# The rotation of q and k in an encoder kernel, on GpSimd instead of VectorE

## The chip, the cores and the metric

One core of one Trainium2 chip runs the whole program. The metric is the device time in microseconds (us), the median of several executions. The engines are named as the profile names them: PE (TensorE's matmuls), PEld (its weight loads), DVE (VectorE), ACT (ScalarE), POOL (GpSimd), SP (SyncE, which here only issues transfers).

## The reference, cut to what matters

Two residual layers (`DEPTH = 2`) over 256 tokens of width 1024. Each layer normalises its input, multiplies it by one wide matrix `w_in`, and feeds the segments of the product to two branches: a gated delta rule (segments `q_a`, `k_a`, `v_a`, with a short convolution) and a differential softmax attention (`q_b`, `k_b`, `v_b`). Both are gated, projected, merged and projected again. The change concerns the attention's `q_b` and `k_b` alone. Before the scores are formed, the first 16 of the 64 columns of each of 16 sub-heads are rotated by an angle that depends on the token:

```python
def partial_rope(t, cos, sin):
    half = ROPE_DIM // 2                     # 8
    x1 = t[..., :half]
    x2 = t[..., half:ROPE_DIM]
    return jnp.concatenate([x1 * c - x2 * s, x2 * c + x1 * s, t[..., ROPE_DIM:]], axis=-1)

q = partial_rope(q.reshape(bsz, seq, DIFF_HEADS, 2, DIFF_DH), cos, sin) * (DIFF_DH ** -0.5)
k = partial_rope(k.reshape(bsz, seq, DIFF_HEADS, 2, DIFF_DH), cos, sin)
```

## The kernel before, in words

All weights come from memory in blocks of 256 rows by 512 columns, `raw`, and each is split into two numbers whose sum it is: `hi`, a cast on ACT (L308; on DVE for the blocks listed as `turned`), and `lo`, a subtraction on DVE (L310). PE multiplies three times, hi by hi, lo by hi and hi by lo. In `proj_tm` (token-major, 512 columns at a time) these are L324, L325 and L326, in `proj_fm` (feature-major, for the convolution) L385, L387 and L389. PE thus waits for ACT's cast and DVE's subtraction of every block.

`qk_part(s_, i)` makes one half (512 columns, `i` = 0 or 1) of q (`s_` = 0) or k (`s_` = 1). `proj_tm` calls `evac_qk(m, ps)` for each of the two tiles of 128 tokens. That makes 2 layers x 2 x 2 x 2 = 16 tiles. For one tile:

- ACT copies the product from the accumulator to `st` (the tile `stg`, 128x512; L597). `st` has two buffers, and the tag is shared with a few other tiles.
- Four operations rotate it in place: two products with cosines and sines into the scratch tile `r4` (L602, L603; 128 elements per partition each), then a difference and a sum back into the first 16 columns of each group of 64 (L604, L605; 64 elements each, in runs of 8). `r4` has one buffer, so the next tile's L602 waits for this tile's L605. In the profile `r4` is called `r`.
- PE transposes the tile in four blocks (L608) into the bank `qkt`, and ACT writes it, scaled, to `qkT` (L610), which the scores (L1061) read later.

The four halves are made between the segments of the other branch: q half 0 after the first half of the convolution of q, q half 1 after its second half, k half 0 and 1 after the first half of the convolution of v and around the second. While the rotation of a half runs, PE is already in the products of the next segment. Around these places DVE also carries out the convolution's taps (L679, L690) and a substitution (L870, L871), which solves the triangular systems.

POOL has other work there: `turn_blocks` sends the blocks of `A` through memory (transfers L847, L849, L850) and clears `X` (L851, L852); `bounce` sends v's squares, after a transposition on DVE (L135), through memory (L140 out, L142 back). A transfer that POOL issues stands in POOL's queue, and what stands behind it waits until it is issued.

Every engine carries out its instructions in the order in which they stand in its queue. That order is not written out in the source: a scheduler sets it while the program is built, from its own estimates of how long each operation takes, within limits that the source gives (`behind(...)` means issued after a certain instruction, `high_priority` moves work forward).

Of the kernel before, what the change touches and what calls it, by code (L numbers as in the profile page):

```python
# [12 lines left out]
ALU = mybir.AluOpType  # L13
# [36 lines left out]
def hybrid_encoder(  # L50
# [19 lines left out]
    V, S, G, T = nc.vector, nc.scalar, nc.gpsimd, nc.tensor  # L70
# [15 lines left out]
    def bank(name):  # L86
        return ps_m.tile([P, 512], F32, tag="m", name=name)
# [10 lines left out]
    def mid(ap, n):  # L98
        return ap.unsqueeze(1).to_broadcast([ap.shape[0], n] + list(ap.shape[1:]))
# [215 lines left out]
    def proj_tm(act, w, c0, n, evac, nm, places=(None,) * 4, spare=(), later=None, turned=(), between=None,  # L315
                banks=None, held=None, first=(), raws={}):

        accs = (banks or banks2)(f"pp_{nm}")
        for kt, hi, lo in weights(w, c0, n, nm, places, later=later, spare=spare, turned=turned, held=held,
                                  first=first, raws=raws):  # L320
            for m in range(NM):
                ts_ = slice(m * P, (m + 1) * P)
                o = accs[m][:, :n]
                T.matmul(o, act[kt // 4][:, 0, kt % 4, ts_], hi, start=kt == 0, stop=False)  # L324
                T.matmul(o, act[kt // 4][:, 0, kt % 4, ts_], lo, start=False, stop=False)  # L325
                mark["proj"] = T.matmul(o, act[kt // 4][:, 1, kt % 4, ts_], hi, start=False,  # L326
                                        stop=kt == KT - 1).ins
                mark["done", nm, kt] = mark["proj"]
        if between:
            between()  # L330
        for m in range(NM):
            evac(m, accs[m][:, :n])
# [174 lines left out]
    for l in range(DEPTH):  # L507
# [26 lines left out]
        if l == 0:  # L534
# [23 lines left out]
            sin, cos = sincos[:, 0], sincos[:, 1]  # L558
# [35 lines left out]
        def qk_part(s_, i):  # L594
                def evac_qk(m, ps):
                    st = work.tile([P, 512], F32, tag="w2a", name=f"stg{l}{s_}{i}{m}", bufs=2)
                    S.copy(st, ps)  # L597
                    g_ = st.rearrange("p (g e) -> p g e", e=DH)
                    x12 = g_[:, :, 0 : 2 * RD].rearrange("p g (x r) -> p g x r", x=2)
                    both = lambda t_: mid(mid(t_[:, m, :], 2), 8)  # L600
                    r4 = small.tile([P, 2, 8, 2, RD], F32, tag="r4", name=f"r4{l}{s_}{i}{m}", bufs=1)
                    V.tensor_tensor(r4[:, 0], x12, both(cos), ALU.mult)  # L602
                    V.tensor_tensor(r4[:, 1], x12, both(sin), ALU.mult)  # L603
                    V.tensor_tensor(x12[:, :, 0], r4[:, 0, :, 0], r4[:, 1, :, 1], ALU.subtract)  # L604
                    V.tensor_tensor(x12[:, :, 1], r4[:, 0, :, 1], r4[:, 1, :, 0], ALU.add)  # L605
                    pt = bank(f"qkt{l}{m}{s_}{i}")
                    for b in range(4):
                        T.transpose(pt[:, b * P : (b + 1) * P], st[:, b * P : (b + 1) * P], ident)  # L608

                    mark["qkT", m] = S.mul(qkT[i][:, s_, :, m * P : (m + 1) * P],  # L610
                                           pt.rearrange("p (b t) -> p b t", b=4), (DH ** -0.5, 1.0)[s_]).ins
                proj_tm(hT, wl, (C_QB, C_KB)[s_] + 512 * i, 512, evac_qk, f"qk{l}{s_}{i}",
                        turned=(0, 1) if (s_, i) == (0, 1) else ())
# [770 lines left out]
```

## Time and profile before

| | |
|---|---|
| median of 3 executions | 749.98 us (749.95 to 750.64) |
| span of the profiled execution, first to last instruction | 748.5 us |
| PE busy | 739.3 us, 99% |
| PEld busy | 641.7 us, 86% |
| DVE busy | 586.5 us, 78% |
| ACT busy | 481.2 us, 64% |
| POOL busy | 139.5 us, 19% |
| mean granted TensorE clock | 0.998 |

The profile holds one execution. Its span runs from the first to the last instruction; the time of an execution includes what lies around that, and the median is 1.5 us above the span. Busy time is the time in which an engine had an instruction; an engine off the chain that ends last may be idle at no cost. Matmuls overlap, so one takes longer (0.39 us for 512 columns) than the distance to the next (0.23 us).

### The profile page before, as it was taken

Reading aid. Unit: us, or ns where it says so; the run is one execution under the profiler, and the core shown is the slowest. Engines: PE = TensorE matmul, PEld = TensorE weight load, DVE = VectorE, ACT = ScalarE, POOL = GpSimd, SP = SyncE. Lnnn points to the kernel's source line nnn. Section 1 sums busy time; section 2 is a strip of 40 time slices with the busy share of each in tenths; the row PEclk is TensorE's granted clock in tenths of the full one; section 3 lists DMA queues with packets and bytes.
Section 4 is the critical chain, followed back from the end, with each engine's and each line's share of the span. In section 5 each row is a group of like instructions: output and inputs, shape, how many; then the busy total and the mean of one; then the engine's idle time right before and its main releaser. Section 6 shows DMA issues by size and latency. Waiting matters only on the chain.

```text
span 748.5 us, 13917 instructions
## 1 busy us (share of the span) xinstructions
PE 739.3 (99%) x5176; PEld 641.7 (86%) x5176; DVE 586.5 (78%) x1109; ACT 481.2 (64%) x1022; POOL 139.5 (19%) x221
## 2 busy tenths in 40 slices
PE   8999999999999999999999999999999999999996
PEld 6999889987888889888889899889778888998885
DVE  8696898999985965578668779999999679537782
ACT  6757875667876576645456578555687757566552
POOL 6004110112023440100000150202110425301000
PEclk9999999999999999999999999999999999999999
DMA  8754566776667462567674466767666748335641
GB/s 260 239 170 169 170 179 198 209 211 193 208 177 186 145 184 84 171 200 247 199 232 133 128 192 180 219 176 230 195 171 195 197 133 229 95 114 201 220 141 57
DMA packets 73734, 135.46 MB, mean 181 GB/s; under 512 B 12944, under 2 KB 13921, under 8 KB 73666
## 3 DMA queue, kind: packets, MB, share of 16 engines
q1 hardware_dynamic: 64750, 113.65, 50.6%
q0 software_dynamic: 7936, 19.35, 8.7%
q10 hardware_dynamic: 980, 1.58, 0.6%
q8 instruction: 41, 0.67, 0.4%
q14 instruction: 27, 0.22, 0.1%
HBM read 125.53 MB, written 9.01 MB: 180 GB/s over the span
## 4 chain that ended last, share of the span: by engine, by line
PE 95%; ACT 2%; issue 1%; DVE 1%; DMA 1%; SPq 0%; POOLq 0%; POOL 0%; DVEq 0%; ACTq 0%
PE pp_vb L369 4%; PE pp_qk L325 4%; PE pp_qk L326 3%; PE pp_qk L324 3%; PE sc L1061 2%; PE pp_o L369 2%; PE pf_k L385 2%; PE pp_za L325 2%; PE pf_v L385 2%; PE pf_v L389 2%; PE pp_gb L324 2%; PE pp_gb L325 2%; PE pp_zb L324 2%; PE pf_q L387 2%; PE pf_k L387 2%; PE pf_v L387 2%
## 5 line engine op out<-in xcount | busy, mean ns | idle before, releaser
L325 PE MATMUL pp_qk<-lo_qk,hT 128*128 128x512 f32 x128 | 50.5, 395 | 0.3
L326 PE MATMUL pp_qk<-hi_qk,hT 128*128 128x512 f32 x128 | 50.0, 390 | 0.0
L310 DVE TENSOR_TENSOR lo_qk<-raw_qk,hi_qk 128x1024 fp32r<-128x1024 f32 x32 | 39.1, 1222 | 11.6 <-ACT hi_qk L308 11.4
L324 PE MATMUL pp_qk<-hi_qk,hT 128*128 128x512 f32 x128 | 45.1, 393 | 0.0
L308 ACT CAST hi_qk<-raw_qk 128x1024 fp32r<-128x1024 f32 x28 | 29.4, 1049 | 23.4 <-PE pp_qk L326 12.4
L1071 ACT ACTIVATE es<-sc,mx 128x256 f32<-128x256 f32 x64 | 29.6, 474 | 19.5 <-DVE mx L1069 19.5
L387 PE MATMUL pf_q<-hT,hi_q 128*128 128x256 f32 x128 | 36.1, 286 | 0.0
L385 PE MATMUL pf_k<-hT,hi_k 128*128 128x256 f32 x128 | 36.1, 287 | 0.0
L385 PE MATMUL pf_v<-hT,hi_v 128*128 128x256 f32 x128 | 35.9, 285 | 0.0
L387 PE MATMUL pf_v<-hT,hi_v 128*128 128x256 f32 x128 | 35.8, 284 | 0.0
L385 PE MATMUL pf_q<-hT,hi_q 128*128 128x256 f32 x128 | 35.8, 284 | 0.0
L387 PE MATMUL pf_k<-hT,hi_k 128*128 128x256 f32 x128 | 35.8, 284 | 0.0
L310 DVE TENSOR_TENSOR lo_pb<-raw_pb,hi_pb 128x1024 fp32r<-128x1024 f32 x16 | 19.6, 1225 | 20.5 <-ACT hi_pb L308 20.2
L389 PE MATMUL pf_q<-hT,lo_q 128*128 128x256 f32 x128 | 35.2, 288 | 0.0
L389 PE MATMUL pf_v<-hT,lo_v 128*128 128x256 f32 x128 | 34.6, 288 | 0.0
L389 PE MATMUL pf_k<-hT,lo_k 128*128 128x256 f32 x128 | 34.3, 284 | 0.0
L308 ACT CAST hi_pa<-raw_pa 128x1024 fp32r<-128x1024 f32 x16 | 16.8, 1053 | 22.3 <-PE pp_pa L326 16.1
L679 DVE SCALAR_TENSOR_TENSOR cvq<-pf_q,cw,cvq 128x254 f32<-128x254 f32 (+1 forms) x64 | 30.0, 479 | 0.9 <-ACT cvq L675 0.3
L679 DVE SCALAR_TENSOR_TENSOR cvv<-pf_v,cw,cvv 128x254 f32<-128x254 f32 (+1 forms) x64 | 30.1, 482 | 0.1
L679 DVE SCALAR_TENSOR_TENSOR cvk<-pf_k,cw,cvk 128x254 f32<-128x254 f32 (+1 forms) x64 | 29.0, 478 | 1.3 <-ACT cvk L675 0.6
L325 PEld LDWEIGHTS pp_qk<-lo_qk,hT 128*128 128x128 f32 x128 | 24.0, 188 | 6.6 <-DVE lo_qk L310 1.6
L310 DVE TENSOR_TENSOR lo_pa<-raw_pa,hi_pa 128x1024 fp32r<-128x1024 f32 x16 | 19.6, 1224 | 11.1 <-ACT hi_pa L308 11.1
(414 smaller groups left out, 2542.2 us busy)
## 6 DMA issues: line engine op xcount, KB each, us to landing
raw_qk<-in_w_in_dram SPq DMA_DIRECT2D x32, 512.0 KB, 3.8
raw_k<-in_w_in_dram SPq DMA_DIRECT2D x16, 512.0 KB, 4.7
raw_q<-in_w_in_dram SPq DMA_DIRECT2D x16, 512.0 KB, 3.7
raw_v<-in_w_in_dram SPq DMA_DIRECT2D x16, 512.0 KB, 3.8
raw_zb<-in_w_in_dram SPq DMA_DIRECT2D x16, 512.0 KB, 3.7
raw_za<-in_w_in_dram SPq DMA_DIRECT2D x16, 512.0 KB, 3.7
raw_ga<-in_w_in_dram SPq DMA_DIRECT2D x16, 512.0 KB, 4.4
raw_pb<-in_w_pb_dram SPq DMA_DIRECT2D x16, 512.0 KB, 3.8
```

The source lines that it names most:

```text
L308: high = (V.tensor_copy if kp in turned else S.copy)(hi[:, :, :n], raw[:, :, :n]).ins
L310: mark[nm, kp] = high, V.tensor_tensor(lo[:, :, :n], raw[:, :, :n], hi[:, :, :n].bitcast(F32), ALU.subtract).ins
L324: T.matmul(o, act[kt // 4][:, 0, kt % 4, ts_], hi, start=kt == 0, stop=False)
L325: T.matmul(o, act[kt // 4][:, 0, kt % 4, ts_], lo, start=False, stop=False)
L326: mark["proj"] = T.matmul(o, act[kt // 4][:, 1, kt % 4, ts_], hi, start=False, stop=kt == KT - 1).ins
L369: mark["proj"] = T.matmul(o, act[kt // 4][:, pa, kt % 4, ts_], ws[kt][1 + pw], start=kt == 0 and n_ == 0, stop=kt == KT - 1 and n_ == 2).ins
L385: T.matmul(o, hi[:, cs], act[kt // 4][:, 0, kt % 4, :], start=first, stop=False, skip_group_check=True)
L387: T.matmul(o, hi[:, cs], act[kt // 4][:, 1, kt % 4, :], start=False, stop=False, skip_group_check=True)
L389: T.matmul(o, lo[:, cs], act[kt // 4][:, 0, kt % 4, :], start=False, stop=done, skip_group_check=True)
L679: V.scalar_tensor_tensor(ca[:, o0:o1], acc[:, b, o0 + sft : o1 + sft], cw[:, j, cb : cb + 1], ca[:, o0:o1], ALU.mult, ALU.add)
L1061: mm = T.matmul(sp[n][:, qt * SEQ : (qt + 1) * SEQ], qkT[h // 4][rows, 0, h % 4, qt * P : (qt + 1) * P], qkT[h // 4][rows, 1, h % 4, :], s ...
L1071: S.activation(es[:, n, qt, :], spv[:, qt, :], AF.Exp, bias=mx[:, n, qt : qt + 1], accum_out=s_all[:, h, n, qt : qt + 1])
```

## The change

The four operations of the rotation are issued by `G` (POOL) and no longer by `V` (DVE). Nothing else in the source is changed.

```diff
                     r4 = small.tile([P, 2, 8, 2, RD], F32, tag="r4", name=f"r4{l}{s_}{i}{m}", bufs=1)
-                    V.tensor_tensor(r4[:, 0], x12, both(cos), ALU.mult)
-                    V.tensor_tensor(r4[:, 1], x12, both(sin), ALU.mult)
-                    V.tensor_tensor(x12[:, :, 0], r4[:, 0, :, 0], r4[:, 1, :, 1], ALU.subtract)
-                    V.tensor_tensor(x12[:, :, 1], r4[:, 0, :, 1], r4[:, 1, :, 0], ALU.add)
+                    G.tensor_tensor(r4[:, 0], x12, both(cos), ALU.mult)
+                    G.tensor_tensor(r4[:, 1], x12, both(sin), ALU.mult)
+                    G.tensor_tensor(x12[:, :, 0], r4[:, 0, :, 0], r4[:, 1, :, 1], ALU.subtract)
+                    G.tensor_tensor(x12[:, :, 1], r4[:, 0, :, 1], r4[:, 1, :, 0], ALU.add)
                     pt = bank(f"qkt{l}{m}{s_}{i}")
```

The scheduler sets a new order on all engines. Two places matter below. First, PE at the transposes of the second tile of k's half 0 in layer 0 (bank `qkt_1724`, tile `stg_1717`), in the products of v's second half (`pf_v`); lines with - stand so before, with + now:

```order
 L389 MATMUL pf_v_1740<-hT_0_126,lo_v_1773 128x256
 L385 MATMUL pf_v_1741<-hT_0_126,hi_v_1772 128x256
+L608 MATMUL qkt_1724<-ident,stg_1717 128x128 x4
 L387 MATMUL pf_v_1741<-hT_0_126,hi_v_1772 128x256
 L389 MATMUL pf_v_1741<-hT_0_126,lo_v_1773 128x256
...
 L385 MATMUL pf_v_1741<-hT_1_127,hi_v_1832 128x256
 L387 MATMUL pf_v_1741<-hT_1_127,hi_v_1832 128x256
-L608 MATMUL qkt_1724<-ident,stg_1717 128x128 x4
 L389 MATMUL pf_v_1740<-hT_1_127,lo_v_1833 128x256
 L385 MATMUL pf_v_1740<-hT_1_127,hi_v_1832 128x256
```

The four transposes stand 33 products earlier than before. Of the other seven sets of transposes in layer 0, one stands where it stood, one stands 5 products later, and five stand earlier, by 1 to 24 rows; among these are the second tile of q's half 0 (`qkt_1117`), 20 products of 256 columns earlier, and the second tile of k's half 1 (`qkt_2012`), 12 products of 512 columns earlier.

Second, POOL's queue at the two tiles of k's half 1 in layer 0 (tiles `stg_1992` and `stg_2005`, scratch `r_1994` and `r_2007`):

```order
 L142 DMA tb_v_1622<-bnc_v_1624 32x4x128 x4
+L602 TENSOR_TENSOR r_1994<-stg_1992,sincos 128x128
+L603 TENSOR_TENSOR r_1994<-stg_1992,sincos 128x128
+L604 TENSOR_TENSOR stg_1992<-r_1994 128x8x8
+L605 TENSOR_TENSOR stg_1992<-r_1994 128x8x8
+L602 TENSOR_TENSOR r_2007<-stg_2005,sincos 128x128
+L603 TENSOR_TENSOR r_2007<-stg_2005,sincos 128x128
 L140 DMA bnc_v_1881<-tb_v_1879 128x512
+L604 TENSOR_TENSOR stg_2005<-r_2007 128x8x8
+L605 TENSOR_TENSOR stg_2005<-r_2007 128x8x8
 L142 DMA tb_v_1879<-bnc_v_1881 32x4x128 x4
```

The second tile's last two operations now stand behind a transfer (L140) that is issued only when DVE has transposed v's squares (L135). In layer 1 both places look the same.

## The prediction

> **What bounds the kernel now.** I read the page's busy times first, then the chain that ended last, then PE's idle time by stages, then what PE waited for.
>
> ```profile
> PE 739.3 (99%) x5176; PEld 641.7 (86%) x5176; DVE 586.5 (78%) x1109; ACT 481.2 (64%) x1022; POOL 139.5 (19%) x221
> PE 95%; ACT 2%; issue 1%; DVE 1%; DMA 1%; SPq 0%; POOLq 0%; POOL 0%; DVEq 0%; ACTq 0%
> 0.00:15.00 15.00, 12.82 (x62) 9.88 (x63) 11.57 (x29) 9.90 (x18) 7.64 (x16) 1.00 0.84 261
> 84.00:175.00 91.00, 91.00 (x565) 80.47 (x565) 85.64 (x182) 60.87 (x120) 13.12 (x23) 1.00 0.69 201
> 450.00:542.00 92.00, 92.00 (x569) 81.31 (x568) 86.64 (x183) 60.92 (x120) 13.12 (x23) 1.00 0.70 202
> 735.00:748.50 13.50, 6.81 (x53) 6.45 (x51) 3.87 (x10) 3.38 (x9) 1.11 (x2) 0.91 0.23 80
> PE pp_vb L464 <- ACT hT L234: 0.6, 1, 0.6
> ```
>
> The rows with a colon are stretches of the span: length, then busy PE, PEld, DVE, ACT and POOL, granted clock, DMA share, GB/s. Of the 748.5 us, PE is idle for 9.2: 2.2 in the first 15 us and 6.7 at the end, where the last rows are normalised and stored. Both rotation stages (84 to 175 in layer 0, 450 to 542 in layer 1) are 100% PE. The waits that the trace lists for PE all lie on lines of the start, the longest but one being the last row above. DVE is nearly full in the rotation stages (85.64 of 91.00 us), but nothing there reaches PE late.
>
> So taking work from DVE gives nothing by itself; what counts is whether anything now reaches PE late.
>
> **What the change removes.**
>
> ```profile
> L602 DVE TENSOR_TENSOR r<-stg,sincos x16: 279/286/297, 87.7 to 529.9; 128x128 f32<-128x128 f32 x16
> L604 DVE TENSOR_TENSOR stg<-r x16: 193/223/230, 88.5 to 532.8; 128x64 f32<-128x64 f32 x16
> ```
>
> (Minimum, median, maximum in ns.) L603 and L605 are like them, so a tile costs DVE 2 x 0.286 + 2 x 0.223 = 1.0 us and all 16 tiles 16 us. That lies beside PE's products. If nothing else moved, the 16 us would turn into idle DVE time and the kernel would not change.
>
> **What it adds on POOL.** No streaming product of two tensors by POOL is in the trace. The nearest rows:
>
> ```profile
> L116 POOL TENSOR_SCALAR_AFFINE_SELECT tri<-tri x2: 282/282/283, 1.6 to 1.9; 128x128 f32<-128x128 f32 x2
> L804 POOL TENSOR_SCALAR_AFFINE_SELECT B<-B x16: 628/640/1613, 64.9 to 437.9; 128x512 f32<-128x512 f32 x16
> L812 POOL TENSOR_TENSOR kds<-B,lnc x8: 191/196/202, 78.6 to 444.9; 128x4 f32<-128x4 f32 x8
> ```
>
> With one input, 128 elements take 282 ns and 512 take 640: 0.93 ns per element on a fixed 163. The lower end for a product is one input's price, 282 and 223 ns, or 1.0 us a tile, as on DVE. For the upper end I take L812, an addition of two inputs: if half of its 196 ns for 4 elements grew with their number, that is 25 ns per element, 128 elements cost 3.2 us, and a tile 9.8. I take twice the one-input slope: 163 + 128 x 1.86 = 401 ns and 163 + 64 x 1.86 = 282 ns, since a slope measured over 128 to 512 elements is nearer to this size than a 4-element row. A tile is then 2 x 0.40 + 2 x 0.28 = 1.37, with a wait for its own result between L603 and L604 (estimate 0.1) 1.5 us.
>
> **How much room there is.** POOL can begin when ACT has copied the tile; PE must find it done at L608, whose new place the order gives. The tightest pair is k's half 0.
>
> ```profile
> 135.55 0.57 ACT L597 COPY stg<-pp_qk 128x512 f32<-128x512 f32 x1
> 137.22 0.57 ACT L597 COPY stg<-pp_qk 128x512 f32<-128x512 f32 x1
> 138.09 1.23 DVE L310 TENSOR_TENSOR lo_v<-raw_v,hi_v 128x1024 fp32r<-128x1024 f32 x1
> 141.02 1.23 DVE L310 TENSOR_TENSOR lo_v<-raw_v,hi_v 128x1024 fp32r<-128x1024 f32 x1
> 145.42 0.28 PE L385 MATMUL pf_v<-hT,hi_v 128*128 128x256 f32 x1
> 145.54 0.28 PE L387 MATMUL pf_v<-hT,hi_v 128*128 128x256 f32 x1
> 145.66 0.60 PE L608 MATMUL qkt<-ident,stg 128*128 128x128 f32 x4
> ```
>
> Products of 256 columns start 0.12 us apart. The second tile's transposes, at 145.66 before, stand 33 products earlier: 145.66 - 33 x 0.12 = 141.7. The first copy ends at 136.1. For the pair's eight operations there are 5.6 us, and they need 3.0. The second tile of q's half 0 stands 20 products earlier:
>
> ```profile
> 88.41 0.57 ACT L597 COPY stg<-pp_qk 128x512 f32<-128x512 f32 x1
> 95.47 0.60 PE L608 MATMUL qkt<-ident,stg 128*128 128x128 f32 x4
> ```
>
> From the copy's end at 89.0 to 95.47 - 20 x 0.12 = 93.1 it has 4.1 us for 1.5.
>
> The other tight place is k's half 1, where the last two operations stand behind the transfer L140:
>
> ```profile
> 165.91 0.72 DVE L135 STREAM_TRANSPOSE tb_v<-thv 128x512 f32<-128x512 f32 x1
> 169.28 0.62 PE L324 MATMUL pp_zb<-hi_zb,hT 128*128 128x512 f32 x2
> 169.74 0.60 PE L608 MATMUL qkt<-ident,stg 128*128 128x128 f32 x4
> L140 POOL DMA_DIRECT2D bnc_v<-tb_v x8 | 4.6, 570 | 98.4 <-DVE stg L605 51.3 <-DVE fstmp L870 30.3 <-DVE tb_v L135 16.8
> ```
>
> PE needs the tile 12 products of 0.23 us earlier, at 169.74 - 2.76 = 167.0. L135 ended at 166.6. DVE had six rotation operations in front of it since 160.0, about 1.1 us by their spacing, which are gone: 165.5. L140 takes 0.57, then L604 and L605 0.56: 166.7, just in time. If DVE gained nothing, it is 167.8 and PE waits 0.8 us, twice (two layers), 1.6 us. Who waits behind a late transpose: all of PE's products.
>
> The transfers that the rotation is moved past cost nothing. L849 and L850 load what this row uses, at 125.2:
>
> ```profile
> L857 DVE COPY la<-lt x2: 1135/1137/1139, 125.2 to 491.2; 64x1024 f32<-64x1024 f32 x2
> 111.74 0.55 POOL L849 DMA_DIRECT2D la<-adr  x1 [3.71 <-DMA adr<-A]
> lt<-adr POOLq DMA_DIRECT2D x2, 256.0 KB, 6.1
> ```
>
> Held up by 1.6 us behind L602 and L603, the second lands near 113.9 + 6.1 = 120, 5 us before its use.
>
> **Where POOL and DVE meet.** One behaviour in the trace speaks against the change.
>
> ```profile
> 67.83 4.96 POOL L804 TENSOR_SCALAR_AFFINE_SELECT B<-B 128x512 f32<-128x512 f32 x6 [1.66 <-DMA B<-gdr]
> 68.10 0.86 DVE L690 SCALAR_TENSOR_TENSOR kq<-thk,cvk 128x256 f32<-128x256 f32 x1
> 69.29 1.23 DVE L310 TENSOR_TENSOR lo_q<-raw_q,hi_q 128x1024 fp32r<-128x1024 f32 x1 [0.33 <-ACT hi_q L308]
> 435.19 1.70 DVE L310 TENSOR_TENSOR lo_q<-raw_q,hi_q 128x1024 fp32r<-128x1024 f32 x1 [0.46 <-ACT hi_q L308]
> L310 DVE TENSOR_TENSOR lo_q<-raw_q,hi_q x16: 1217/1226/1695, 47.9 to 460.3; 128x1024 fp32r<-128x1024 f32 x16
> ```
>
> Six L804 should take 3.8 us and took 4.96, one of them 1.61 instead of 0.64, while L310 ran beside them; L690 took 0.86 (0.43 in a row further down), and one L310 took 1.70 instead of 1.23. So streaming reads by POOL and DVE operations with two inputs from SBUF hold each other up. The Trainium skill (SBUF — State Buffer, "Who interferes with whom") says the same as a rule: such a DVE instruction and a GpSimd instruction that reads SBUF exclude each other, and the second to start is fully blocked. By that rule the rotation would not leave DVE's way at all; the time it would give is the first rival's, worked out from rows below, and the trace agrees with it in these five rows.
>
> ```profile
> 136.17 0.28 DVE L871 TENSOR_TENSOR X<-X,fstmp 128x112 f32<-128x112 f32 x1
> 140.29 0.43 DVE L690 SCALAR_TENSOR_TENSOR thv<-thv,cvv 128x256 f32<-128x256 f32 x1
> ```
>
> In the window of k's half 0 (136.1 to 141.7) DVE has the two L310 quoted above (2.3 us of holding) and, of the short two-input operations, five from the first to the last of these rows (two L690, two L871, one L870; 1.7 us): at most 4.0 us in POOL's way. L679 (an input from PSUM) and L135 (one input) leave it free. I take half, 2.0 us, since POOL can run beside those. Then 3.0 + 2.0 = 5.0 of 5.6 us: in time, by 0.6. On DVE the loss (up to 0.4 us for each of four POOL operations) about eats the 1.0 us a tile that it is rid of; L310 then comes when it came before.
>
> **The sum.** PE's 739.3 us stay, the 9.2 us at both ends stay, at most a few tenths of waits come: span 748.5 + 0.2, and with the 1.5 us between this span and the median, **750.2 us**.
>
> **The rivals.**
>
> *Slower by mutual blocking.* All of DVE's two-input work falls on POOL's operations: 3.0 + 4.0 = 7.0 against 5.6 us, so 1.4 us late at the second tile of each of 8 halves, 11 us, **761**; with 1.0 us lost at half of the places 4 us, **754**. It decides from 2.6 us of blocking in a pair on. For it: DVE is 94% busy there and nobody times the two against each other. Against it: my count is at most 4.0 and L679 fills much of DVE's time.
>
> *Slower because POOL's operations are longer.* At 1.5 times my price a pair needs 4.1 + 2.0 = 6.1 us, 0.5 late, 8 x 0.5 = 4 us, **754**; at double, 5.9 + 2.0 = 7.9, 2.3 late, 18 us, **768**; at the upper end of 9.8 us a tile some 8 x 16 us more, **880**. For it: runs of 8 elements and a repeated angle, which no POOL row has. Against it: L812 reads single elements at a stride and is done in 196 ns.
>
> *Faster.* DVE's relief would have to reach PE. There is no wait between 15 and 735 us of over 0.2 us to remove, so only closer spacing of products could gain: **748**. Against it: the 100% rows.
>
> **How the numbers follow.** Chances: my forecast 0.52, mutual blocking 0.27, longer operations 0.13, faster 0.08. A difference within 0.2% (1.5 us) cannot be told from none here. Faster 0.08, same 0.52, slower 0.40. The forecast's own range is 749.2 to 751.4. The range to hold 8 in 10 goes from 748.6 to 758: below lies about 0.05, above the worse half of the first rival and the far parts of the second, about 0.14.
>
> **What would show it.** Right: PE idle in 84 to 175 and 450 to 542 stays under 0.5 us; L602 on POOL near 0.4 us at its minimum, L604 near 0.28; no row of PE waiting at L608 for POOL; DVE about 16 us less busy, or less than that by what POOL holds it up. Wrong by blocking: minima as forecast but maxima over 1 us, and PE waiting at L608 or, for DVE, at L389 and L325. Wrong by price: minima of 0.6 us and more, with PE waiting at the second tile of each half. If only `qkt` of k's half 1 waits, it is the transfer in front of L604.

## The result and the profile after

The changed kernel takes 752.1 us (median of 16 executions, 751.65 to 753.46), the kernel before, timed beside it, 750.29 (749.76 to 750.75). The ratio, which here and below need not be the quotient of the two medians, is 1.0026, with a 95% interval of 1.0018 to 1.0033: 1.8 us slower, and clear of no change. The forecast was 750.2. The measured time lies outside the forecast's own range (749.2 to 751.4) and inside the wide one that leaves room for the rivals (748.6 to 758). The profiled execution of the changed kernel has a span of 750.3 us.

First the page of the changed kernel, its busy times and the chain that ended last; then the two rotation stages, with the same columns as before; then what PE waited for (total us, times, longest).

```profile
PE 739.9 (99%) x5176; PEld 641.9 (86%) x5176; DVE 583.1 (78%) x1045; ACT 480.8 (64%) x1022; POOL 178.1 (24%) x285
PE 93%; ACT 2%; POOL 1%; issue 1%; DVE 1%; DMA 1%; SPq 0%; POOLq 0%; DVEq 0%; ACTq 0%
```

```profile
84.00:175.00 91.00, 90.33 (x562) 79.92 (x560) 83.72 (x150) 60.58 (x120) 31.90 (x55) 1.00 0.69 199
450.00:542.00 92.00, 91.33 (x566) 80.70 (x566) 84.82 (x153) 61.17 (x121) 33.03 (x55) 1.00 0.69 198
```

```profile
PE qkt L608 <- POOL stg L605: 1.2, 2, 0.6
```

64 instructions left DVE and came to POOL, yet DVE's busy time fell by 3.4 us and not by 16, while POOL's rose by 38.6. PE, which was busy for the whole of both stages, is now idle 0.67 us in each. The last row names what it waits for: PE waits for the rotation twice, once in each layer. POOL has appeared on the chain with 1%.

How long POOL's operations take (minimum, median, maximum in ns), 16 of each line:

```profile
L602 POOL TENSOR_TENSOR r<-stg,sincos x16: 458/474/627, 87.6 to 530.2; 128x128 f32<-128x128 f32 x16
L604 POOL TENSOR_TENSOR stg<-r x16: 317/759/1306, 88.6 to 531.7; 128x64 f32<-128x64 f32 x16
```

The minima are near the price that was forecast. The maximum of L604 is four times its minimum. The timeline shows where: the pair of k's half 0 in layer 0, with ACT's copy of the first tile, POOL, DVE and PE.

```profile
135.69 0.59 ACT L597 COPY stg<-pp_qk 128x512 f32<-128x512 f32 x1 [0.35 <-PE pp_qk L326]
136.42 0.48 POOL L602 TENSOR_TENSOR r<-stg,sincos 128x128 f32<-128x128 f32 x1 [17.45 <-ACT stg L597]
136.87 0.99 POOL L603 TENSOR_TENSOR r<-stg,sincos 128x128 f32<-128x128 f32 x1
137.94 1.31 POOL L604 TENSOR_TENSOR stg<-r 128x64 f32<-128x64 f32 x1
139.21 0.32 POOL L605 TENSOR_TENSOR stg<-r 128x64 f32<-128x64 f32 x1
139.60 0.62 POOL L602 TENSOR_TENSOR r<-stg,sincos 128x128 f32<-128x128 f32 x1
140.19 0.64 POOL L603 TENSOR_TENSOR r<-stg,sincos 128x128 f32<-128x128 f32 x1
140.91 1.30 POOL L604 TENSOR_TENSOR stg<-r 128x64 f32<-128x64 f32 x1
142.17 0.41 POOL L605 TENSOR_TENSOR stg<-r 128x64 f32<-128x64 f32 x1
137.85 1.22 DVE L310 TENSOR_TENSOR lo_v<-raw_v,hi_v 128x1024 fp32r<-128x1024 f32 x1
139.83 0.68 DVE L690 SCALAR_TENSOR_TENSOR thv<-thv,cvv 128x256 f32<-128x256 f32 x1
140.82 1.21 DVE L310 TENSOR_TENSOR lo_v<-raw_v,hi_v 128x1024 fp32r<-128x1024 f32 x1
141.74 0.28 PE L385 MATMUL pf_v<-hT,hi_v 128*128 128x256 f32 x1
142.64 0.66 PE L608 MATMUL qkt<-ident,stg 128*128 128x128 f32 x4 [0.61 <-POOL stg L605]
143.05 0.36 PE L387 MATMUL pf_v<-hT,hi_v 128*128 128x256 f32 x1
```

Both long L604 begin 0.1 us after a subtraction of DVE and end 0.2 us after its record does, though 0.32 us is all they take alone: they stood still while it ran. The pair needs 6.16 us, from 136.42 to 142.58. The transposes stand behind the product that starts at 141.74 and start 0.90 us after it, where the next product would have started after 0.12: 0.78 us lost. Layer 1 repeats it (508.50, then 509.40), so this place costs 2 x 0.78 = 1.56 us of the 1.8. Where the rest comes from was not found.

POOL does not bring this tile later than DVE did. Its last operation in the kernel before:

```profile
143.31 0.23 DVE L605 TENSOR_TENSOR stg<-r 128x64 f32<-128x64 f32 x1
```

There the tile was done at 143.54, now at 142.58, about 1.0 us earlier in spite of the hold. But PE came for it at 145.66 and would now come at 141.86. The tile is late against its new place in PE's order, not against the kernel before.

A second way to see it: take the start of the same product in the traces of before and after and follow the difference, the lag (the median over stretches of 15 us). It is nearly the same for hundreds of us and rises in the two stages with the rotation.

| lag of PE's products against before, us | at 60 | at 255 | at 420 | at 615 | rise in layer 0 | in layer 1 |
|---|---|---|---|---|---|---|
| after | 0.12 | 1.04 | 1.00 | 1.84 | 0.92 | 0.84 |

What precedes the first rotation (0.12 here, between -0.57 and +0.43 in the experiments) arises in the first 15 us of each trace. With one trace of each kernel it cannot be told whether that is scatter from one execution to the next. So each rise, not the span, is the number to compare.

### The profile page after: what moved, and what is told of

Same layout as the page of the kernel before. It is cut to its first block, busy times and chain, and to the rows that moved or that the text cites. A ratio compares the mean times of both kernels' runs of the same rounds, so it can differ in the third digit from the quotient of the medians.

```text
span 750.3 us, 13958 instructions
## 1 busy us (share of the span) xinstructions
PE 739.9 (99%) x5176; PEld 641.9 (86%) x5176; DVE 583.1 (78%) x1045; ACT 480.8 (64%) x1022; POOL 178.1 (24%) x285
## 4 chain that ended last, share of the span: by engine, by line
PE 93%; ACT 2%; POOL 1%; issue 1%; DVE 1%; DMA 1%; SPq 0%; POOLq 0%; DVEq 0%; ACTq 0%
PE pp_vb L369 4%; PE pp_qk L325 3%; PE pp_qk L326 3%; PE pp_qk L324 3%; PE sc L1061 2%; PE pp_o L369 2%; PE pp_za L325 2%; PE pf_k L385 2%; PE pp_zb L324 2%; PE pp_gb L324 2%; PE pp_ga L324 2%; PE pf_q L387 2%; PE pf_k L387 2%; PE pf_k L389 2%; PE pf_q L385 2%; PE pf_q L389 2%
## 5 line engine op out<-in xcount | busy, mean ns | idle before, releaser
L326 PEld LDWEIGHTS pp_qk<-hi_qk,hT 128*128 128x128 f32 x128 | 24.0, 188 | 4.9
```

## The experiments

The theory was: POOL's operations are as cheap as forecast, but they stand still beside DVE's subtractions, and at k's half 0 this makes the second tile late for its transposes. The rivals: the rotation's pattern makes POOL slow, or several halves lose a little each.

Places in PE's order are given as rows. The expectations count them from another start than the text: 43 more (763 there is 720 here).

**All but k's half 0, and only k's half 0.** Two complementary parts of the change:

```diff
+                    R_ = V if (s_, i) == (1, 0) else G
-                    G.tensor_tensor(r4[:, 0], x12, both(cos), ALU.mult)
+                    R_.tensor_tensor(r4[:, 0], x12, both(cos), ALU.mult)
...
```

The other three operations are issued by `R_` as well; in the second kernel the first line reads `G if (s_, i) == (1, 0) else V`.

> The rotation of k's half 0 (both its tiles, both layers) goes back to VectorE, the other 12 tiles stay on GpSimd. Its transposes stand later in PE's order again (row 811 of PE's order for the second tile in layer 0, against 763 in the changed kernel). Place theory (the whole loss is PE's wait of 0.8 us at the second tile of k's half 0, once a layer): no row of PE waiting at the transposes, 750.3 us, ratio to before 1.000 with 0.0005 either way. Price theory (GpSimd's operations are slow everywhere and each tile costs something): 12 of 16 tiles are left, so 1.4 us of the 1.8 stay, 751.7 us. Order theory (some other part of the new order costs the time): 752 us, as in the changed kernel.

> Only the two tiles of k's half 0 are rotated on GpSimd, the other 12 tiles are on VectorE as before. The second tile's transposes stand at row 765 of PE's order in layer 0 (763 in the changed kernel, 796 before). Place theory: two products of 0.12 us later than in the changed kernel, so PE waits 2 x 0.5 to 0.6 us there, 751.3 to 751.5 us. Price theory: 4 of 16 tiles, 0.4 us, 750.7. Order theory: most of the order is that of before, 750.3.

Measured against 750.23 (23 executions of before): all but k's half 0, 751.02 us, ratio 1.0011 (1.0002 to 1.002); only k's half 0, 752.34, ratio 1.003 (1.0019 to 1.0041). PE's wait and the stage of layer 0 with only k's half 0, then both stages without it, where no wait for the rotation is left:

```profile
PE qkt L609 <- POOL stg L606: 0.6, 2, 0.3
```

```profile
84.00:175.00 91.00, 90.69 (x562) 79.66 (x561) 85.48 (x176) 61.33 (x120) 18.99 (x31) 1.00 0.68 200
```

```profile
84.00:175.00 91.00, 90.93 (x563) 80.25 (x563) 85.29 (x162) 61.32 (x120) 28.78 (x48) 1.00 0.68 201
450.00:542.00 92.00, 91.95 (x569) 81.08 (x568) 86.39 (x163) 61.22 (x120) 28.84 (x48) 1.00 0.69 202
```

Four of the 16 tiles bring the whole loss back, twelve bring no wait for the rotation. That is the place theory's pattern, but both times lie above the ones that it gave (750.3, and 751.3 to 751.5). The rises are 0.38 and 0.31 us without k's half 0, and 0.90 and 0.86 with it alone. Not all of that is the wait: of the 0.90, 0.5 come at it, as expected, and most of the rest around k's half 1, where the kernel without k's half 0 has its 0.38 too. There, in layer 0, single products start 0.1 to 0.2 us late, at the first low half of `zb` and at the first tile's transposes; these were not followed further. Since the scheduler sets a new order for every variant, the two parts need not add up to the change (0.8 + 2.1 against 1.8 us), and the expectation that each would behave as its part of the change was too simple.

**The subtraction in halves** (`split_lo`)**.** If L604 waits for one subtraction, a shorter one holds it up less. The subtractions of v's second half are cut in two (all others stay whole; the code is cut):

```diff
+                    if nm in ("v01", "v11"):
+                        for k in range(2):
+                            low = V.tensor_tensor(lo[:, k, :n], raw[:, k, :n],
+                                                  hi[:, k, :n].bitcast(F32), ALU.subtract).ins
+                        mark[nm, kp] = high, low
```

> As the changed kernel, but VectorE's subtraction for the weights of v's second half (4 blocks a layer) is made in two instructions of 512 elements, not one of 1024. If one VectorE instruction holds GpSimd up as long as it lasts (blocking theory), the longest L604 of k's half 0 falls from 1.31 us to about 0.9, since a half lasts about 0.69 us, the pair's eight operations from 6.2 us to about 5.4, and PE's wait, with its transposes 3 products (0.36 us) earlier in the new order, from 0.8 to about 0.4 or less: 751 us. If GpSimd's own duration is what is long, the pair stays at 6.2 us and PE waits 1.1 us a layer: 752.8 us.

Measured: 752.57 us, ratio 1.0035 (1.0022 to 1.0047), rises of 1.20 and 1.22 us. The expected shorter hold did not come at the first tile, as the timeline shows; then PE's waits:

```profile
137.69 1.29 DVE L312 TENSOR_TENSOR lo_v<-raw_v,hi_v 128x512 fp32r<-128x512 f32 x2
137.79 1.37 POOL L610 TENSOR_TENSOR stg<-r 128x64 f32<-128x64 f32 x1
140.82 0.77 POOL L610 TENSOR_TENSOR stg<-r 128x64 f32<-128x64 f32 x1
```

```profile
PE qkt L614 <- POOL stg L611: 1.6, 2, 0.8
```

The first L610 waited for both halves as for one; the second got in between its two. The pair still took 6.1 us (136.20 to 142.32). The transposes meanwhile stood three products earlier in PE's order, at row 717 and not 720, so the wait rose. The time is near the one expected if POOL's own duration were long (752.8 us); against that reading stand the second L610, which took 0.77 us, and POOL's price alone, measured below.

**The transposes later.** The change as it is, with the second tile's transposes of k's half 0 issued 17 rows later in PE's order (row 737). What was a loop in place is now a function `finish`, with the loop of transposes, each now `behind(mark.get("late"))`, and ACT's copy in it, which is called there for all other tiles (cut):

```diff
+            if held_back and nm in ("v01", "v11") and kt == 4:
+                mark["late"] = mark["pf"]
+                held_back.pop()()
+                mark.pop("late")
...
+                    if (s_, i, m) == (1, 0, 1):
+                        held_back.append(finish)
+                    else:
+                        finish()
```

> As the changed kernel, with all rotations on GpSimd, but the transposes of the second tile of k's half 0 are issued behind a later product of v's second half (row 780 of PE's order in layer 0, 17 products or 2.0 us after the place in the changed kernel). Place theory: GpSimd's work and the blocking stay as they are (pair 6.2 us, longest L604 1.3 us), PE does not wait at any transpose, 750.3 us. Price theory: the same, so this run alone does not tell them apart. Order theory: the loss stays, 752 us.

Measured: 749.9 us, ratio 1.0001 (0.9992 to 1.0009), rises of -0.03 and -0.12 us, no wait for the rotation. From the timeline, the end of the pair and the transposes; then the stages:

```profile
140.18 1.30 POOL L610 TENSOR_TENSOR stg<-r 128x64 f32<-128x64 f32 x1
141.45 0.41 POOL L611 TENSOR_TENSOR stg<-r 128x64 f32<-128x64 f32 x1
143.16 0.60 PE L616 MATMUL qkt<-ident,stg 128*128 128x128 f32 x4
```

```profile
84.00:175.00 91.00, 90.95 (x568) 80.68 (x567) 83.16 (x153) 61.54 (x121) 32.20 (x55) 1.00 0.67 197
450.00:542.00 92.00, 91.95 (x572) 81.50 (x572) 84.27 (x154) 61.52 (x121) 32.27 (x55) 1.00 0.69 198
```

POOL is held up just as before (the pair takes 6.17 us, and L610 again 1.30), but 1.3 us lie between the end of the pair and the transposes. So the hold alone costs nothing; it costs where the order has PE come too soon. This version is as fast as the kernel before, not faster, which is what a PE without gaps leads one to expect.

**Only one tile given back.** DVE makes the second tile of k's half 0, POOL all others (`R_ = V if (s_, i, m) == (1, 0, 1) else G`).

> The changed kernel with one tile in eight given back to VectorE: the second token tile of k half 0, in both layers. Theory (the second tile of this pair is the one whose turn comes too soon): no wait of TensorE before the turns of q and k, the lag of TensorE's products against the kernel before grows by under 0.4 us per layer instead of 0.9, and the time is 750.2 to 751.1 us. Rival (the first tile's delay shifts everything behind it on VectorE, so that the second is as late wherever it is made): the wait stays at 0.3 to 0.6 us in each layer and the time at 751.5 to 752.5.

Measured: 751.06 us against 750.25, ratio 1.0012 (1.0002 to 1.0021), rises of 0.24 and 0.06 us, no wait for the rotation. The theory's numbers hold, but its reason does not. DVE's last operation on the tile, and its transposes:

```profile
142.74 0.22 DVE L606 TENSOR_TENSOR stg<-r 128x64 f32<-128x64 f32 x1
145.61 0.60 PE L609 MATMUL qkt<-ident,stg 128*128 128x128 f32 x4
```

DVE is done with it at 142.96, no sooner than POOL in the changed kernel (142.58). But the scheduler has moved the transposes 29 rows back, to row 749, and PE comes for the tile at 145.61. So this run does not separate the engine from the place; it agrees with the run before, in which the place alone was moved. The same is true of "all but k's half 0": there DVE is done at 144.51, and PE comes at 147.23, row 768. Of the 0.8 us that the version with one tile given back loses, the rises show 0.3; another 0.43 stand in its trace before the first rotation, and their cause is open.

**What POOL's operations cost, and what holds them up.** A small program with nothing of the encoder in it:

> Not the encoder: a small program that measures the disputed cost alone, and leaves all of the computation out (it copies x to the output). Stages: GpSimd alone, four flat products of 128 elements and four tiles' worth of rotation with the kernel's own access patterns (runs of 8, repeated angle); VectorE alone, four each of the subtraction (two inputs from SBUF, 1024 elements), the convolution's tap (one input from PSUM, one from SBUF, 256) and a copy (one input from SBUF, 1024); then the rotation beside back-to-back subtractions, beside taps, and beside copies. Blocking theory: 0.46 and 0.32 us alone; beside subtractions nearly every operation is longer, up to 1.6 us, and the subtractions are longer too; beside taps 0.46 and 0.32 with no change on either side. Price theory: the same durations in all stages. Pattern theory (the runs of 8 make it dear): the flat product of 128 elements takes clearly less than 0.46 us. Beside copies: open; the trace of the kernel does not say whether a copy with one input holds GpSimd up.

The price first, POOL alone: a flat product, and the rotation's difference in runs of 8. Then the stage with eight subtractions beside POOL: DVE's group (busy us, mean ns), and POOL's timeline, whose first instruction there copies one element:

```profile
L54 POOL TENSOR_TENSOR f_a<-fl x4: 452/453/453, 1.8 to 3.0; 128x128 f32<-128x128 f32 x4
L47 POOL TENSOR_TENSOR o_a<-r_a x4: 317/318/319, 4.4 to 8.8; 128x64 f32<-128x64 f32 x4
```

```profile
L60 DVE TENSOR_TENSOR lo_c<-a,b 128x1024 fp32r<-128x1024 f32 x8 | 9.2, 1216 | 0.0
```

```profile
18.20 9.12 POOL L79 COPY mg_c<-cp_b 128x1 f32<-128x1 f32 x1 [8.66 <-DVE cp_b L72]
27.28 0.45 POOL L45 TENSOR_TENSOR r_c<-st,cs 128x128 f32<-128x128 f32 x1
```

The product takes 0.45 us flat and 0.45 with the rotation's pattern, so the pattern costs nothing and that rival falls. The copy of one element, 0.18 us alone, was held until the last of the eight subtractions had ended, and DVE lost nothing (1216 ns each, 1219 alone). Beside DVE's taps, which read PSUM, neither side was delayed. Beside twelve copies of 1024 elements POOL was again held to the end, for 7.26 us. In both stages the rotation itself thus began only when DVE had ended, so this program does not show it beside subtractions or copies.

That a whole row of subtractions can hold POOL, and not just one, led to the next program:

> A small program that leaves out the whole encoder and copies parts of x to the output; it only runs GpSimd's rotation tiles and VectorE's subtractions side by side, in stages c to e and g, after stages in which each engine is alone. It asks what lets GpSimd in between VectorE's subtractions. Theory (run holding): GpSimd is kept out as long as VectorE's holding instructions follow one another without a gap, whatever their length, and gets in at the first instruction that does not hold. By it: stage c (twelve subtractions of 512 back to back, about 0.65 us each) GpSimd's first instruction is held for about all twelve, some 7 us, as it was for eight of 1024; stage d (subtractions of 1024, each followed by a tap of 0.47 us from PSUM) GpSimd's instructions end one or two per tap, none over 1.6 us, and the four tiles are done when about six pairs of VectorE are; stage e (the same with a fill of 256 elements in place of the tap) is like c if a fill holds too and like d if it does not. Rival (single wait): GpSimd waits for the end of one VectorE instruction only, and the long holds seen before were the start of a stage; then in c its instructions take at most 0.65 + 0.45 = 1.1 us each. Stage g (GpSimd first, with multiplications of 1024 of some 2.2 us, VectorE's subtractions coming in behind): if the hold works both ways, VectorE's first subtraction takes up to 2 us more than its 1.22; if only VectorE holds, it stays at 1.22 and GpSimd's multiplications wait.

First groups (minimum, median, maximum in ns): DVE's subtractions of 512, alone and twelve of them beside POOL, and POOL's long products in the stage that POOL begins. Then the timeline: POOL's first instructions beside the twelve, two of POOL's in the stage with a fill behind each subtraction, and DVE's copy behind POOL's long product:

```profile
L92 DVE TENSOR_TENSOR ha_b<-a,b x4: 684/686/693, 5.2 to 7.1; 128x512 fp32r<-128x512 f32 x4
L92 DVE TENSOR_TENSOR ha_c<-a,b x12: 683/868/941, 13.5 to 21.9; 128x512 fp32r<-128x512 f32 x12
L110 POOL TENSOR_TENSOR lg_g<-a,b x4: 2337/2826/3318, 53.4 to 61.3; 128x1024 f32<-128x1024 f32 x4
```

```profile
14.17 0.91 POOL L45 TENSOR_TENSOR r_c<-st,cs 128x128 f32<-128x128 f32 x1
15.05 0.90 POOL L46 TENSOR_TENSOR r_c<-st,cs 128x128 f32<-128x128 f32 x1
...
38.52 1.18 POOL L47 TENSOR_TENSOR o_e<-r_e 128x64 f32<-128x64 f32 x1
39.66 1.38 POOL L48 TENSOR_TENSOR o_e<-r_e 128x64 f32<-128x64 f32 x1
...
53.47 2.29 DVE L118 COPY vs_g<-gs_g 128x8 f32<-128x8 f32 x1
```

The theory of the long hold failed for the halves: there the engines took turns, POOL's instructions 0.65 to 0.91 us and DVE's 0.87 instead of 0.69, as the rival had it. With a fill or a tap behind each subtraction POOL got in at every one. In the last stage POOL held DVE: a copy of 8 elements took 2.29 us beside a product of 2.34, and the subtractions behind it a median of 3.36 us instead of 1.22. So the exclusion works both ways, and in these stages POOL got in wherever a tap or a fill came between. Whether it also gets in between two holding instructions back to back is not settled: it did for twelve subtractions of 512 and once in `split_lo`, it did not for eight of 1024, for twelve copies, nor the other time in `split_lo`.

**A fill between the halves.** If that is so, the pair gets shorter in the kernel too when something that does not hold stands between the halves (the code is cut, and compared with the version in halves):

```diff
                         for k in range(2):
+                            if k:
+                                tc.keep_in_program_order(V.memset(lo[:, 1, :256].bitcast(F32), 0.0))
                             low = V.tensor_tensor(lo[:, k, :n], raw[:, k, :n],
-                                                  hi[:, k, :n].bitcast(F32), ALU.subtract).ins
+                                                  hi[:, k, :n].bitcast(F32), ALU.subtract)
+                            tc.keep_in_program_order(low)
```

> The changed kernel, with the low-half subtraction of v's second half cut into two of 512 elements per block, as in split_lo, and a fill of 256 elements (0.27 us, overwritten by what follows) between the two; the fill and whatever VectorE does next to it now stand between the halves. Theory (GpSimd waits for as long as VectorE's holding instructions follow one another, and gets in where one that doesn't hold comes between): the longest half-width instruction (0.32 us alone) falls from 1.3 us to at most 0.32 + 0.65 = 0.97, the pair of k half 0 takes at most 5.6 us instead of 6.1 and 6.2, and TensorE's wait before the turn of its second tile falls from 0.8 to under 0.4 us; time 750.2 to 751.5. Rival (the second tile is late since its first instruction starts late, whatever holds it): the longest instruction falls, but the wait stays above 0.6 us in each layer and the time at 751.7 to 752.6, the fills' 0.27 us in eight places being VectorE's and not TensorE's.

Measured: 753.14 us against 750.17, ratio 1.0045 (1.0029 to 1.0062), rises of 1.44 and 1.08 us. POOL's first instruction of the pair, a former long one and the last, PE's two sets of transposes, and PE's wait:

```profile
135.75 0.60 POOL L612 TENSOR_TENSOR r<-stg,sincos 128x128 f32<-128x128 f32 x1 [17.46 <-ACT stg L607]
137.30 0.32 POOL L614 TENSOR_TENSOR stg<-r 128x64 f32<-128x64 f32 x1
139.67 0.50 POOL L615 TENSOR_TENSOR stg<-r 128x64 f32<-128x64 f32 x1
138.80 0.60 PE L618 MATMUL qkt<-ident,stg 128*128 128x128 f32 x4
140.22 0.66 PE L618 MATMUL qkt<-ident,stg 128*128 128x128 f32 x4 [0.82 <-POOL stg L615]
```

```profile
PE qkt L618 <- POOL stg L615: 1.6, 2, 0.8
```

The half of the theory that concerns POOL holds in this pair: it takes 4.4 us (135.75 to 140.17) and no longer 6.16, less than the time that it had in the changed kernel. The half that concerns PE does not, and not for the rival's reason either. PE waits just as long because the scheduler has moved the second tile's transposes forward again, to row 705, directly behind those of the first at row 704.

The time is above both expectations (751.5 and 752.6 at most). Of the rise of 1.44 us in layer 0, 0.9 come at these transposes and 0.3 at 152 us, where the first product with a low half of k's half 1 (L335) starts late; the rest was not followed.

All versions side by side, for the second tile of k's half 0 in layer 0: the row of its transposes, when the tile is done, when PE comes for it (behind the instruction ahead of it at the usual distance), and the wait that the profile lists (some 0.2 us less than the time lost):

| version | tile made on | row | done, us | PE comes, us | wait, us |
|---|---|---|---|---|---|
| all but k's half 0 | DVE | 768 | 144.51 | 147.23 | none |
| before | DVE | 753 | 143.54 | 145.66 | none |
| one tile given back | DVE | 749 | 142.96 | 145.61 | none |
| transposes later | POOL | 737 | 141.86 | 143.16 | none |
| only k's half 0 | POOL | 722 | 142.23 | 141.81 | 0.3 |
| the change | POOL | 720 | 142.58 | 141.86 | 0.6 |
| subtraction in halves | POOL | 717 | 142.32 | 141.41 | 0.8 |
| fill between the halves | POOL | 705 | 140.17 | 139.2 | 0.8 |

In no version is the tile done later on POOL than on DVE (the traces are shifted against each other by up to 1.0 us). What decides is the row together with the hold: an unheld pair, 3.1 us from 136.42, would be done at 139.5, in time for the new place too. That is worked out, not run.

What would have happened with the shorter pair and the transposes at row 720 was not tried.

## Why the prediction was right or wrong

**What bounds the kernel: right.** PE had no room; 0.8 of the lag's 0.9 us in layer 0 come where PE waits for the rotation, and DVE's relief brought nothing.

**The price on POOL: right.** Forecast 0.40 and 0.28 us and 3.0 for a pair; alone, two tiles took 3.02 us from first start to last end (1.68 to 4.70 in the second small program). The rows have 0.45 and 0.32, but neighbours overlap: starts lie 0.41 and 0.28 apart. The rival of longer operations has fallen. Its own sums were not made alike: the 4.1 us leave out the wait between operations, the 5.9 double it; with the wait once a tile they are 4.3 and 5.7.

**The room: right.** Forecast 5.6 us from ACT's copy to the transposes; it was 5.58 (the copy's end at 136.28 to 141.86, one product behind the row at 141.74). POOL began 0.14 us after the copy's end.

**The blocking: wrong, and the step that failed.** "I take half, 2.0 us", of at most 4.0. In the kernel an undisturbed tile takes 1.55 us (second tile of q's half 0 in layer 0), a pair 3.1, so 6.16 - 3.1 = 3.06 us were blocking. The two subtractions alone account for 1.0 each: L604, 0.32 when free, took 1.31 and 1.30. Half of the rest is L603 of the first tile, 0.99 instead of 0.46. The argument for half was that POOL can run beside the instructions that leave it free. It can, but it works through its queue in order: when its next operation is ready just behind the start of a subtraction, it stands for the rest of it, whatever gaps come later. Pair and place together gave "in time, by 0.6"; it was 0.7 late. The threshold of the first rival, 2.6 us of blocking, was passed.

**The first rival, in kind but not in size.** Its mechanism decided, but at one of four halves in each layer and with 0.78 us, not at all eight with 1.4 or at four with 1.0. The other pairs had more room: the second tile of q's half 0 was done at 91.77 and needed at 93.25, that of k's half 1 at 166.47 and needed at 168.05. It was close once more: in layer 1 the q tile was held too (L605 took 1.40 us) and was done 0.4 us before its place (459.62 and 460.00). It would have been better to give each half its own price from its own room and leave the uniform sum.

**The transfer at k's half 1 and the moved loads: no loss**, as forecast; the tile behind L140 was 1.6 us early.

**What DVE gets back: right in direction.** The loss "about eats" the relief: 3.4 us are left of 16 by durations. The largest L690 of `thv` is 0.68 us, 0.44 before. How much of the rest is blocking and how much is overlap of neighbouring records was not separated.

**The sum.** "At most a few tenths of waits" should read 2 x 0.78 = 1.56 us; 750.29 + 1.56 = 751.85, against 752.1 measured. That the wide range holds the result owes something to luck: it reached so far for rivals priced at four or eight late places and 754 us or more, and one late place a layer falls between them and the forecast. Of the signs listed, the third (no PE wait at L608) and the first (idle under 0.5 us in a stage) failed, and the one for "wrong by blocking" came in full: minima as forecast, maxima over 1 us, PE waiting at L608.

## What to carry to other kernels

When work is moved to an engine that shares something with the old one, price each place by its own room, and take an operation that is ready just behind a long holding instruction as held for the whole of it: 1.0 us per subtraction here, not a share. Then look at what the new order asks of the result. Here the tile came about 1.0 us earlier than before, but its transposes were moved 33 rows, 4 us, forward; with the fill the pair got shorter and the transposes were moved forward again. That the scheduler does so because it does not know of the hold is likely, but was not shown. So where such a move must cost nothing, fix the place of the consumer as well; with it 17 rows later the loss was gone.

## What the runs showed of the hardware

The exclusion of DVE and POOL, for which the prediction named the Trainium skill (SBUF — State Buffer, "Who interferes with whom"), can be longer than one instruction: a one-element copy by POOL stood for 9.12 us behind eight subtractions, and for 7.26 us behind twelve copies of 1024 elements with one input from SBUF. So one input is not by itself a reason for leaving POOL free, as the prediction had it for the transposition L135, though L135 did leave it free (L605 of the first tile took 0.32 us beside it). It works both ways (2.29 us for DVE's copy of 8 elements beside a product of POOL). Taps with one operand in PSUM and fills left POOL free. Strided runs of 8 elements and a repeated operand cost POOL nothing against a flat product, 0.45 us for 128 elements in both.
